# A hybrid decoder layer on one core: seven-product pairs in ten more column units, single wide splits, a denser state-space branch and branch results kept in DRAM

## The chip, the cores and the metric

The kernel runs on one core of a Trainium2 chip. Its engines are named as in the profile: PE (matrix multiply, with PEld for its weight loads), DVE (element-wise work on two inputs), ACT (element-wise work on one input, functions), POOL and SP; SP, ACT and POOL can issue DMAs, and each issues in the order of its own queue. The metric is the time of one execution in microseconds; the time of a kernel is the median of several.

## The reference

One decoder layer for 256 tokens of width 4096, in float32, and a final norm. What is computed, cut to its frame:

```python
def hybrid_layer(x, ln_g, w_in, ..., branch_g, w_out):
    h = rmsnorm(x, ln_g)
    proj = h @ w_in                                    # 4096 x 12288
    p_x, p_gate, q, k, v, a_gate, s_u, s_gate = split(proj)
    y_pool = pool_mixer(p_x, w_pool, pool_scale)       # causal pooling, 1024 wide
    y_attn = stick_breaking_attention(q, k, v)         # 16 heads, 2048 wide
    y_ssm = s5_mixer(s_u, ..., w_glu, b_glu)           # state space, 1024 wide, then GELU and h @ w_glu (1024 x 2048)
    y = concatenate([rmsnorm(y_pool, g_pool) * silu(p_gate),
                     rmsnorm(y_attn, g_attn) * silu(a_gate),
                     rmsnorm(y_ssm, g_ssm) * silu(s_gate)])
    return x + y @ w_out                               # 4096 x 4096
# and rmsnorm(., final_g) of the result
```

## The kernel before, in words

**Units and pairs.** The three weight matrices are cut into units of 512 columns: 24 of `w_in`, 4 of `w_glu`, 8 of `w_out`. `IN_ORDER` gives the order: two each of `su`, `px`, `pg`, `sg`; then `v`, `q`, `k` three times; the four `glu`; `v`, `q`, `k` once more; four `ag`; then eight `out`. A unit walks over its rows in pairs of 128-row blocks: 16 pairs in an `in` or `out` unit, 4 in a `glu` unit, 528 pairs in all (`N_SUB`). The weights of a pair, 512 KB, come by one DMA from SP into one of four buffers `w` (`load`).

**Three products for float32.** A pair's weights are split into a rounded part `hi` (ACT, a copy to fp32r) and a remainder `lo` (DVE, a subtraction), here one 128-row block (128x512) at a time, with five buffers each (`split`). The stationary operand, `xhl`, is split in the same way. `mm_tok` multiplies hi by hi, hi by lo and lo by hi for both halves of the tokens: 12 matmuls of 512 columns a pair.

**Seven products for four.** In the pairs 2, 5, 7, 9 and 11 of each `out` unit (`SEVEN`) the 2 x 2 block product over two token halves and two 256-column halves is formed from seven block products instead of eight. `sums_seven` makes four sums of weight blocks on DVE and splits them (`sums7`), one pair ahead of the pair's own split (`SUMS_AHEAD`); `split_seven` splits the raw blocks; `mm_seven` issues 7 x 3 matmuls of 256 columns; four of the seven go to PSUM tiles of their own, which `join_seven` adds up once a unit. Sums of the rows of `xhl` that they need are made by `sums_of_rows` during the last `ag` unit.

**Side work.** The state-space branch (`ssm`, on the DVE above all) and the other branches' work are generators. The main loop advances `side_q` by three steps a pair, and `ssm_q` by `SSM_RATE` = 1.5 steps a pair from pair 30 on; a scheduler that works offline turns the order in the program into a fixed order for each engine, and moves an instruction ahead of others where it expects it to be ready. SP is left out of that: its DMAs are issued in program order. Results of branches stay in SBUF: `ypT`, `ysT`, `yaT`, `ao`, `sgate`, `uT`.

**The hand-over to the output projection.** After the last `ag` unit, `finish` refills `xhl` with the branch results, one block at a time:

```python
if n == 3:
    for i in range(28):
        hi_lo(xhl[:, i, 0, :], xhl[:, i, 1, :], y_src(i))
```

A block can be refilled as soon as the last `ag` unit has used it. The four blocks left come straight from `att_gate`'s last call (`direct`).

**The end.** The last four pairs (`HELD`) are multiplied for the first token half at once and for the second half later, so that the first half's final norm lies beside matmuls.

Of the kernel before, what the change touches and what calls it, by code (L numbers as in the profile page):

```python
# [19 lines left out]
P = 128  # L20
L = 256
# [10 lines left out]
HELD = 4  # L32
WARM = 8
SUMS_AHEAD = 1
SEVEN = (2, 5, 7, 9, 11)
SQUARE_AT = (0, 1, 3, 4, 6, 7, 9, 10)
SSM_FROM = 30
SSM_RATE = 1.5
# [18 lines left out]
def body(tc, a, out, ctx):  # L57
    nc = tc.nc
    V, S, T = nc.vector, nc.scalar, nc.tensor
# [17 lines left out]
    bp = pool("base")  # L77
    pm = pool("pmain", space=PSUM)
# [14 lines left out]
    def act(o, x, f, **kw):  # L93
        S.activation(o, x, f, **kw)  # L94
# [8 lines left out]
    xt0 = bp.tile([P, 2, L], F32, tag="k4", bufs=6, name="xt")  # L103
# [25 lines left out]
    wtiles, htiles = {}, {}  # L129
    held = []  # L130
# [13 lines left out]
    def hi_lo(dst_hi, dst_lo, src):  # L144
        act(dst_hi, src, AF.Copy)
        tt(dst_lo, src, dst_hi.bitcast(F32), ALU.subtract)

    def seven(i):
        return i < N_SUB and subs[i][1] in SEVEN and units[subs[i][0]][0] == "out"

    def sums_seven(i):
        w = wtiles[i]
        left, right = w[:, :, 0:L], w[:, :, L:2 * L]
        t = bp.tile([P, 4, L], F32, tag="k4", bufs=6, name="t7")
        tt(t[:, 0:2, :], right, w[:, 0, :].rearrange("p (c m) -> p c m", c=2), ALU.subtract)
        tt(t[:, 2, :], right[:, 1, :], t[:, 0, :], ALU.subtract)
        tt(t[:, 3, :], left[:, 1, :], t[:, 2, :], ALU.subtract)
        sums = bp.tile([P, 2, 4, L], F32R, tag="k8", bufs=3, name="sums7")
        hi_lo(sums[:, 0], sums[:, 1], t)
        htiles[i] = sums  # L160

    def split_seven(i):
        w = wtiles.pop(i)
        raw = []
        for kk in range(2):
            n = L if kk == 0 else NU
            hi = wp.tile([P, NU], F32R, tag="hi", bufs=5, name="hi")
            lo = wp.tile([P, NU], F32R, tag="lo", bufs=5, name="lo")
            hi_lo(hi[:, 0:n], lo[:, 0:n], w[:, kk, 0:n])
            raw.append((hi, lo))  # L170
        htiles[i] = (raw, htiles[i])

    def mm_seven(i, s, ps, pp):
        (b11, b2), sums = htiles.pop(i)
        xa, xb, y = xhl[:, 2 * s], xhl[:, 2 * s + 1], state["s7"][s]
        lo_half, hi_half = slice(0, P), slice(P, L)
        first = s == SEVEN[0]
        last = s == SEVEN[-1]
        for o, stat, mov, begin, end in (
            (pp[0], xa[:, :, lo_half], [v[:, 0:L] for v in b11], first, last),  # L180
            (ps[:, 0, 0:L], xb[:, :, lo_half], [v[:, 0:L] for v in b2], False, False),
            (ps[:, 0, L:2 * L], y[:, 2], [v[:, L:2 * L] for v in b2], False, False),
            (pp[1], y[:, 0], [sums[:, h, 0] for h in range(2)], False, last),
            (pp[3], xa[:, :, hi_half], [sums[:, h, 1] for h in range(2)], first, last),
            (pp[2], y[:, 1], [sums[:, h, 2] for h in range(2)], False, last),
            (ps[:, 1, 0:L], xb[:, :, hi_half], [sums[:, h, 3] for h in range(2)], False, False),
        ):
            for k, (p, q) in enumerate(((0, 0), (0, 1), (1, 0))):
                T.matmul(o, stat[:, p, :], mov[q], start=begin and k == 0, stop=end and k == 2, skip_group_check=True)  # L189

    def join_seven(pp, xr):
# [839 lines left out]
```

## Time and profile before

| | |
|---|---|
| median of 3 runs | 1538.15 us (1537.11 to 1541.42) |
| the profiled execution | 1538.15 us, its span 1536.4 us |
| granted TensorE clock | 0.998 |
| PE busy | 1521.1 us |
| DVE busy | 1186.9 us |
| ACT busy | 931.6 us |
| moved by DMA | 308.22 MB, 201 GB/s on average |

Busy time is the union of an engine's instructions. A matmul's row shows the start and a modelled end; successive matmuls overlap, so what one costs is read from the distance of two starts. In a row of the list of waits stand the engine, line and tile that waited, what released it, and then the sum, the number and the longest of the waits in microseconds.

### The profile page before, as it was taken

To read this page: it belongs to the slowest core of one execution; us is meant where nothing else is said; L and a number is where in the kernel's file an instruction comes from. 1 tells how busy PE (TensorE), PEld (TensorE's weight loads), DVE (VectorE), ACT (ScalarE), POOL (GpSimd) and SP (SyncE) were. 2 spreads that over 40 slices of the span, in tenths; PEclk is the share of its full clock that TensorE was granted. 3 is DMA by queue.
4 is the path that set the end of the run, shared out by engine and by line. 5 is a ranking of instruction groups with operands and counts; after the bars stand their busy time and mean duration, and the time that the engine had idled before them with its cause. 6 is when DMAs were issued, how large, how long until landed. Compare 5 with 4: busy or idle time off the path is not lost.

```text
span 1536.4 us, 21621 instructions
## 1 busy us (share of the span) xinstructions
PE 1521.1 (99%) x7328; PEld 1266.3 (82%) x7328; DVE 1186.9 (77%) x2304; ACT 931.6 (61%) x1677; POOL 0.2 (0%) x4
## 2 busy tenths in 40 slices
PE   9999999999999999999999999999999999999996
PEld 7888788878788888788888888888888888888885
DVE  7579878999899879897645744555677988888886
ACT  7765556766566655575546755456677655555554
POOL 0000000000000000000000000000000000000000
PEclk9999999999999999999999999999999999999999
DMA  9866655665656556554655555555655666666665
GB/s 336 310 220 202 194 179 187 196 209 185 209 187 196 189 165 200 189 179 159 191 192 178 182 185 189 192 164 178 192 183 187 218 221 213 223 210 206 216 215 199
DMA packets 94351, 308.22 MB, mean 201 GB/s; under 512 B 11808, under 2 KB 17696, under 8 KB 94240
## 3 DMA queue, kind: packets, MB, share of 16 engines
q1 hardware_dynamic: 84096, 295.92, 58.5%
q10 hardware_dynamic: 10144, 10.92, 2.5%
q8 instruction: 57, 0.93, 0.3%
q14 instruction: 54, 0.44, 0.1%
HBM read 299.45 MB, written 4.19 MB: 198 GB/s over the span
## 4 chain that ended last, share of the span: by engine, by line
PE 96%; DVE 2%; DMA 1%; ACT 0%; issue 0%; SPq 0%; DVEq 0%; ACTq 0%
PE pm L242 29%; PE pm L241 28%; PE pm L243 28%; PE ps L189 3%; PE pm L189 2%; DMA w<-in_ws 1%; PE ps_y L562 1%; PE ps_c L658 1%; DVE lo L82 1%; PE ps_bu L535 1%; PE ps_z L588 0%; PE ps_p L346 0%; PE ps_t L286 0%; DVE t L82 0%; PE ps_z L606 0%; DVE sums L82 0%
## 5 line engine op out<-in xcount | busy, mean ns | idle before, releaser
L82 DVE TENSOR_TENSOR lo<-w,hi 128x512 fp32r<-128x512 f32 (+1 forms) x1048 | 697.5, 680 | 272.5 <-ACT hi L232 266.3
L232 ACT ACTIVATE hi<-w 128x512 fp32r<-128x512 f32 x968 | 602.3, 629 | 455.0 <-PE pm L243 270.0
L242 PE MATMUL pm<-lo,xhl 128*128 128x512 f32 x1872 | 732.7, 391 | 0.2 <-DVE lo L82 0.2
L241 PE MATMUL pm<-hi,xhl 128*128 128x512 f32 x1872 | 730.9, 391 | 1.1 <-ACT xhl L94 0.6
L243 PE MATMUL pm<-hi,xhl 128*128 128x512 f32 x1872 | 731.0, 391 | 0.0
L241 PEld LDWEIGHTS pm<-hi,xhl 128*128 128x128 f32 x1872 | 351.8, 188 | 75.1 <-ACT hi L232 1.7
L242 PEld LDWEIGHTS pm<-lo,xhl 128*128 128x128 f32 x1872 | 351.8, 188 | 74.4 <-issue 2.9
L243 PEld LDWEIGHTS pm<-hi,xhl 128*128 128x128 f32 x1872 | 351.8, 188 | 71.2 <-issue 0.8
L91 DVE SCALAR_TENSOR_TENSOR et<-et,pw,tr 128x16 f32<-128x16 f32 (+3 forms) x256 | 56.2, 277 | 1.5 <-ACT tr L94 1.3
L94 ACT ACTIVATE sums<-t 128x1024 fp32r<-128x1024 f32 x40 | 42.3, 1057 | 24.6 <-DVE t L82 24.6
L82 DVE TENSOR_TENSOR sums<-t,sums 128x1024 fp32r<-128x1024 f32 x40 | 48.9, 1223 | 9.2 <-ACT sums L94 9.2
L94 ACT ACTIVATE hi<-w 128x256 fp32r<-128x256 f32 x80 | 40.0, 518 | 23.4 <-PE pm L243 19.7
L94 ACT ACTIVATE tr<-et,pw 128x32 f32<-128x32 f32 (+3 forms) x128 | 45.4, 386 | 9.6 <-DVE et L91 5.5
L189 PE MATMUL ps<-sums,s 128*128 128x256 f32 x240 | 46.8, 285 | 0.9 <-DVE sums L82 0.9
L82 DVE TENSOR_TENSOR t<-w 128x512 f32<-128x512 f32 x40 | 27.6, 690 | 22.0 <-DMA w<-in_ws 21.9
L550 DVE TENSOR_TENSOR_SCAN tb<-rho,ta 128x256 f32<-128x256 f32 x64 | 40.7, 680 | 0.1
L189 PEld LDWEIGHTS ps<-sums,s 128*128 128x128 f32 x240 | 36.7, 192 | 1.7 <-DVE sums L82 1.5
L82 DVE TENSOR_TENSOR t<-w,t 128x256 f32<-128x256 f32 x80 | 33.7, 421 | 0.3
L94 ACT ACTIVATE sgm<-sgm 128x1024 f32<-128x1024 f32 x24 | 25.3, 1052 | 0.2
L243 PE MATMUL pm<-hi,hhl 128*128 128x512 f32 x64 | 25.3, 395 | 0.0
L242 PE MATMUL pm<-lo,hhl 128*128 128x512 f32 x64 | 25.2, 393 | 0.0
L241 PE MATMUL pm<-hi,hhl 128*128 128x512 f32 x64 | 25.1, 392 | 0.0
(259 smaller groups left out, 1123.7 us busy)
## 6 DMA issues: line engine op xcount, KB each, us to landing
w<-in_ws SPq DMA_DIRECT2D x527, 512.0 KB, 3.4
xsq<-in_xr SPq DMA_DIRECT2D x8, 512.0 KB, 6.5
xr<-in_xr SPq DMA_DIRECT2D x8, 512.0 KB, 4.5
xt<-in_xT SPq DMA_DIRECT2D x15, 256.0 KB, 6.0
b<-in_bst ACTq DMA_DIRECT2D x16, 192.0 KB, 3.8
u<-uT ACTq DMA_DIRECT2D x96, 32.0 KB, 2.6
out<-o SPq DMA_DIRECT2D x6, 512.0 KB, 4.1
fg<-in_fg SPq DMA_DIRECT2D x8, 256.0 KB, 5.5
```

The source lines that it names most:

```text
L82: V.tensor_tensor(o, x, y, op)
L91: V.scalar_tensor_tensor(o, x, s, y, op0, op1)
L94: S.activation(o, x, f, **kw)
L189: T.matmul(o, stat[:, p, :], mov[q], start=begin and k == 0, stop=end and k == 2, skip_group_check=True)
L232: made = S.activation(hi, w[:, kk, :], AF.Copy)
L241: T.matmul(ps[t], stat[:, slot, 0, sl], hi, start=first, stop=False)
L242: T.matmul(ps[t], stat[:, slot, 0, sl], lo, start=False, stop=False)
L243: T.matmul(ps[t], stat[:, slot, 1, sl], hi, start=False, stop=last)
L535: T.matmul(ps[:, c, :], b3r[:, j, c, :], u3r[:, j, :], start=c == 0, stop=True, skip_group_check=True)
L550: V.tensor_tensor_scan(tb[:, c, :], rho[:, pr:pr + 1].broadcast_to([P, L]), ta[:, c, :], 0.0, ALU.mult, ALU.add)
L562: T.matmul(ps[32 * j:32 * j + 32, 0:L], cf[:, j, c, :], ss[j][:, c, :], start=c == 0, stop=c == 1, skip_group_check=True)
L658: T.transpose(ps[:, (c * 2 + t) * P:(c * 2 + t + 1) * P], z[:, t, (h * 2 + c) * P:(h * 2 + c + 1) * P], ident)
```

## The change

1. Seven-product pairs: six of 16 pairs, in each `out` unit (`SEVEN_OUT`) and now also in the `in` units from the fifteenth on (`SEVEN_IN`, `SEVEN_FROM`): the last two groups of `v`, `q`, `k` and the four `ag`, ten units. For these the rows' sums come from `x`, loaded again (`load_again`, `sums_of_x`) during the unit before. The four separate PSUM tiles of an `in` unit take the second buffers of the main PSUM tiles.
2. The last `v`, `q`, `k` group moves ahead of `glu`. `SSM_RATE` becomes 1.75, and the state-space branch must be complete at the start of unit 13 (`start_late`; unit 16's end before).
3. A pair is split in one instruction of ACT and one of DVE (128x1024), in a ring of four buffers (`RING`); the sums of a seven-product pair take a second buffer of the ring and are split when the pair is, no longer one pair ahead. The sums themselves are made one pair ahead, as before.
4. Branch results go to DRAM from POOL's queue (`kept`, `aout`, `sgate`) and come back: seven groups by `take_back` from SP after the last `ag` unit, with the rows' sums made there; the others from POOL.
5. Main PSUM tiles are one per token half. The tail scales the output in four pieces instead of five; the held pairs stay in the ring.

```diff
+RING = 4
+K4 = 8
 SUMS_AHEAD = 1
-SEVEN = (2, 5, 7, 9, 11)
+SEVEN_FROM = 14
+SEVEN_IN = (0, 3, 5, 8, 10, 12)
+SEVEN_OUT = (1, 3, 6, 8, 10, 12)
-SSM_RATE = 1.5
+SSM_RATE = 1.75
+    + [("v", V0 + 1536), ("q", Q0 + 1536), ("k", K0 + 1536)]
     + [("glu", n) for n in (1024, 0, 1536, 512)]
-    + [("v", V0 + 1536), ("q", Q0 + 1536), ("k", K0 + 1536)]
...
+    def ring():
+        return [wp.tile([P, 4 * L], F32R, tag=k, bufs=RING, name=k) for k in ("hi", "lo")]
...
     def sums_seven(i):
+        w = wtiles[i].rearrange("p k n -> p (k n)")
+        b12, b11, b22, b21 = (w[:, q * L:q * L + L] for q in range(4))
+        t = bp.tile([P, 4, L], F32, tag="k4", bufs=K4, name="t7")
+        tt(t[:, 0, :], b12, b11, ALU.subtract)
+        tt(t[:, 1, :], b22, b12, ALU.subtract)
+        tt(t[:, 2, :], b22, t[:, 0, :], ALU.subtract)
+        tt(t[:, 3, :], b21, t[:, 2, :], ALU.subtract)
+        stiles[i] = t
+    def split(i):
...
+        w = wtiles.pop(i).rearrange("p k n -> p (k n)")
+        raw = ring()
+        at = L if seven(i) else 0
+        for n in (slice(0, NU), slice(NU, 2 * NU)) if i == 0 else (slice(at, 2 * NU),):
+            made = hi_lo(raw[0][:, n], raw[1][:, n], w[:, n])
+        if seven(i):
+            sums = ring()
+            hi_lo(sums[0], sums[1], stiles.pop(i).rearrange("p q m -> p (q m)"))
...
+        for o, stat, mov, start, stop in (          # mm_seven
+            (pp[0], xa[:, :, lo_half], b11, begin, False),
+            (pp[1], y[:, 0], t0, False, end),
+            (pp[3], xa[:, :, hi_half], t1, begin, False),
+            (pp[2], y[:, 1], t2, False, end),
+            (ps[0][:, L:2 * L], xb[:, :, lo_half], b21, first, False),
+            (ps[0][:, 0:L], y[:, 2], b22, False, False),
+            (ps[1][:, L:2 * L], xb[:, :, hi_half], t3, first, False),
...
+    def row_sums(s, xa, xb):
+        t = state["rows"].tile([P, 3, P], F32, tag="t", bufs=1, name="ts")
+        tt(t[:, 0, :], xa[:, P:L], xb[:, P:L], ALU.add)
+        tt(t[:, 1, :], t[:, 0, :], xa[:, 0:P], ALU.subtract)
+        tt(t[:, 2, :], xb[:, 0:P], t[:, 1, :], ALU.subtract)
+        y = state["rows"].tile([P, 3, 2, P], F32R, name="y7_%d" % s)
+        hi_lo(y[:, :, 0, :], y[:, :, 1, :], t)
+    def row_difference(xa):
+        tt(xa[:, P:L], xa[:, 0:P], xa[:, P:L], ALU.subtract)
+    def sums_of_x(s):
+        xs = xtiles.pop(s)
+        for j in range(2):
+            act(xs[:, j, :], xs[:, j, :], AF.Copy, scale=ln_g[:, 2 * s + j:2 * s + j + 1])
+        row_sums(s, xs[:, 0, :], xs[:, 1, :])
+        row_difference(xs[:, 0, :])
+        hi_lo(xhl[:, 2 * s, 0, P:L], xhl[:, 2 * s, 1, P:L], xs[:, 0, P:L])
+    def take_back(g):
+        t = bp.tile([P, 4, L], F32, tag="k4", bufs=K4, name="yk")
+        nc.sync.dma_start(t, kept[g])
+        for h in range(2):
+            s = 2 * g + h
+            if s in SEVEN_OUT:
+                row_sums(s, t[:, 2 * h, :], t[:, 2 * h + 1, :])
+                row_difference(t[:, 2 * h, :])
+        hi_lo(xhl[:, 4 * g:4 * g + 4, 0, :], xhl[:, 4 * g:4 * g + 4, 1, :], t)
...
     def scaled(ps, name):
+        e = state.pop("joined", None)
+        if e is not None:
+            times_r(e, [e[:, t, :] for t in range(2)])
+            tt(z, z, e, ALU.add)
...
             if n == 3:                               # finish, "ag"
-                for i in range(28):
-                    hi_lo(xhl[:, i, 0, :], xhl[:, i, 1, :], y_src(i))
+                for g in range(7):
+                    take_back(g)
...
+            if ui == SEVEN_FROM - 1:                 # main loop, s == 0
+                start_late()
+                state["rows"] = lp
+        if these and s == these[0]:
+            if kind != "out":
+                pz = [pm.tile([P, 2, L], F32, tag="c%d" % t, bufs=2, name="p7") for t in range(2)]
```

More of the change, by code (lines that the diff above doesn't have):

```diff
@@ L162, in split_seven @@
[L162 to L174, printed above, removed]
+        if i >= N_SUB:
+            return False
@@ L247, in body @@
+    state = {"s7": {}}
     xtiles = {}
@@ L363, in pool_gate, with uT @@
         y = ypool.pop(u)
[L364 to L368 removed]
+        yield from transposed(y, keep(u))
+    u_parts = [bp.tile([P, 4, L], F32, tag="k4", bufs=K4, name="uT") for _ in range(2)]
+    def uT(ct):
+        return u_parts[ct // 4][:, ct % 4, :]
+    glu, sgate = {}, {}
     def ssm_params(sp, k):
@@ L738, in start_end @@
         state["o"] = ep.tile([P, 2, D], F32, name="o")
-    def y_src(i):
-        return ypT[:, i, :] if i < 8 else state["ysT"][:, i - 8, :] if i < 16 else state["yaT"][:, i - 16, :]
     def start_out(n):
```

321 lines of the change are left out of this document (146 added, 175 removed).

## The prediction

> **What bounds the kernel now.** First the page's busy times, then the list of waits of PE alone, whole.
>
> ```profile
> span 1536.4 us, 21621 instructions
> PE 1521.1 (99%) x7328; PEld 1266.3 (82%) x7328; DVE 1186.9 (77%) x2304; ACT 931.6 (61%) x1677; POOL 0.2 (0%) x4
> ```
>
> ```profile
> PE ps_i L111 <- DVE zeros L108: 1.2, 1, 1.2
> PE ps L189 <- DVE sums L82: 0.9, 2, 0.5
> PE pm L241 <- DVE o L82: 0.8, 1, 0.8
> PE pm L241 <- ACT xhl L94: 0.6, 1, 0.6
> ...
> PE pm L242 <- DVE lo L82: 0.2, 1, 0.2
> ```
>
> PE is fed from end to end: it waits some 4 us in 1536. So a cut in PE's work counts in full as long as DVE, ACT and the weight DMAs keep delivering, and what they cannot deliver comes back as a wait of PE. How much room they have is read stage by stage (busy time of PE, PEld, DVE, ACT, POOL in each stretch, then clock and DMA):
>
> ```profile
> 100.00:735.00 635.00, 635.00 (x2963) 518.28 (x2963) 559.03 (x1251) 387.68 (x720) 0.00 (x0) 1.00 0.59 189
> 735.00:1137.00 402.00, 402.00 (x1849) 334.91 (x1848) 230.87 (x357) 233.15 (x391) 0.00 (x0) 1.00 0.58 185
> 1180.00:1222.50 42.50, 41.98 (x239) 36.77 (x238) 37.59 (x64) 28.13 (x47) 0.00 (x0) 1.00 0.63 209
> 1307.50:1350.00 42.50, 42.50 (x238) 37.20 (x237) 36.13 (x59) 24.67 (x42) 0.00 (x0) 1.00 0.66 216
> ```
>
> The rows are the stage with the state-space branch, the input units behind it, the first output unit and a later one. DVE is at 88%, 57%, 88% and 85%; ACT has room everywhere. DVE is the engine that can become the bound.
>
> **1. The added seven-product pairs.** What a matmul costs is the distance of starts:
>
> ```profile
> 1420.08 0.28 PE L189 MATMUL ps<-sums,xhl 128*128 128x256 f32 x1
> ...
> 1421.76 0.52 PE L189 MATMUL pm<-sums,xhl 128*128 128x256 f32 x3
> ...
> 1430.60 0.39 PE L243 MATMUL pm<-hi,xhl 128*128 128x512 f32 x1
> ...
> 1439.67 0.39 PE L241 MATMUL pm<-hi,xhl 128*128 128x512 f32 x1
> ```
>
> Between the first two rows lie 14 starts, 1.68/14 = 0.120 us for 256 columns; between the last two 40 starts, 9.07/40 = 0.2268 us for 512. A plain pair is 12 x 0.2268 = 2.722 us, a seven-product pair 21 x 0.120 = 2.520: 0.202 us saved, 7%, not an eighth, because 256 columns cost more than half of 512. Before there are 8 x 5 = 40 such pairs, after it 8 x 6 + 10 x 6 = 108. 68 x 0.202 = 13.7 us. That is the whole gain; the other edits make room for it. (Between 13 and 14.5, if the distances move by 1%.)
>
> The Trainium skill, "TensorE: Matmul & The Clock Gate", section "Back-to-back issue gap", gives N/2.4 + 2.5 ns for isolated warm matmuls. By it the distances would be 109 and 216 ns, a pair would save 0.29 us and the 68 pairs 20 us. The trace disagrees: 0.120 and 0.2268 are both about 11 ns over that formula, which 21 matmuls pay more often than 12, so the measurement decides.
>
> **2. DVE's bill for them.** DVE instructions too are priced by the distance of starts:
>
> ```profile
> 1405.46 1.23 DVE L82 TENSOR_TENSOR sums<-t,sums 128x1024 fp32r<-128x1024 f32 x1 [0.19 <-ACT sums L94]
> 1406.60 0.69 DVE L82 TENSOR_TENSOR t<-w 128x512 f32<-128x512 f32 x1
> 1407.20 0.69 DVE L82 TENSOR_TENSOR lo<-w,hi 128x512 fp32r<-128x512 f32 x1
> 1407.80 0.42 DVE L82 TENSOR_TENSOR t<-w,t 128x256 f32<-128x256 f32 x1
> 1408.14 0.69 DVE L82 TENSOR_TENSOR lo<-w,hi 128x512 fp32r<-128x512 f32 x1
> ```
>
> 1024 columns cost 1.14 us, 512 cost 0.60, 256 cost 0.34; so some 0.07 each and 0.267 for 256 columns, and by estimate from these 0.87 for 768, 0.47 for 384, 0.20 for 128. A plain pair's remainder falls from 1.20 to 1.14. A seven-product pair costs 4 x 0.34 + 0.87 + 1.14 = 3.37 (before: 0.60 + 2 x 0.34 + 1.14 + 0.60 + 0.34 = 3.36). An output unit is then 10 x 1.14 + 6 x 3.37 = 31.6 against 11 x 1.20 + 5 x 3.36 = 30.0 before: +1.6 on 36.13, so 37.7 in a unit that PE does in 42.3, 89%. An input unit with six pairs has 31.6 and the joining, 4 x 0.34 + 1.14 = 2.5, and its side work: 57% becomes some 85%. On average DVE holds, and this step costs nothing by itself.
>
> **3. The shorter warning for sums.** Their split moves behind the pair's own and shares a ring of four. Where two such pairs stand two apart (3, 8, 10, 12 of an output unit; 5, 10, 12 of an input unit: 8 x 4 + 10 x 3 = 62 cases) the sums' buffer is the one that the raw blocks of the former pair free three matmuls before that pair ends, and the sums are wanted after three matmuls of the next one: 0.36 + 2.72 + 0.36 = 3.44 us for ACT's split and DVE's.
>
> ```profile
> L94 ACT ACTIVATE sums<-t 128x1024 fp32r<-128x1024 f32 x40 | 42.3, 1057 | 24.6 <-DVE t L82 24.6
> L94 ACT ACTIVATE kz<-pm,rtok 128x512 f32<-128x512 f32 x8 | 5.1, 686 | 2.2 <-PE pm L243 2.2
> ```
>
> 1.06 + 1.23 leave 1.15 us; a single ACT instruction of 1.06 us ahead uses that up. Nothing to 0.4 us a case, 0 to 25 us. I take 1 us in all, near the lower end: before, the same sums made PE wait twice in 40 pairs (0.9 us).
>
> **4. PSUM of the input units.** The separate tiles take the second buffers, so at ten unit starts pair 0 or its like waits until ACT has emptied the unit before: the second token half is emptied after the unit's last matmul, 0.69 us (row of `kz`). Six matmuls of the first token half's tiles (0.72 us) and, in an order that the scheduler may choose, nine on the main tiles can run ahead of it. 0 to 10 x 0.69 = 7 us; I take 1, since the matmuls ahead cover the evacuation unless ACT is late.
>
> **5. The hand-over to the output units.** Here the change moves work onto the path. Before, the refill of `xhl` runs inside the last input unit, block by block behind PE:
>
> ```profile
> 1138.15 0.42 DVE L82 TENSOR_TENSOR xhl<-ypT,xhl 128x256 fp32r<-128x256 f32 x1
> ...
> 1175.85 0.42 DVE L82 TENSOR_TENSOR xhl<-yaT,xhl 128x256 fp32r<-128x256 f32 x1
> ```
>
> ```profile
> 1179.91 1.27 ACT L94 ACTIVATE agz<-pm,rtok 128x512 f32<-128x512 f32 x2 [0.15 <-PE pm L243]
> ```
>
> All 28 blocks are nearly done when that unit ends (`agz`, 1179.9). After the change the data must come back first, and `take_back`'s seven DMAs stand on SP behind the weights of the fourth output pair, whose buffer comes free only when the last input pair is split.
>
> ```profile
> w<-in_ws SPq DMA_DIRECT2D x527, 512.0 KB, 3.4
> SPq L141 <- DVE lo L82: 1037.3, 423, 6.6
> ```
>
> SP waits there in nearly every pair. That split waits for the ring buffer which pair 12 frees, three plain pairs or 8.2 us before the end; the first group is issued some 5.8 us before it and lands, with 3.4 us, 2 to 3 us before it. So nearly all the work falls into the first output unit: 7 x 1.14 + 6 x (3 x 0.20 + 0.47 + 0.20) = 15.6 us of DVE. With the 37.59 us that DVE does in this unit now and 1.6 more, it is 54.8 us against 42.3: 12.5 too many. Against it stand the lead of the ring (two to three pairs, some 4 us of DVE work that may be eaten up) and one group done early (2.4): 6 us are left for PE to wait. From 0 (all refills find gaps) to 13 (no lead, and the seven loads, which hold the next weights back on SP, land late). I take 6, the sum.
>
> **6. The state-space branch.** It must end before pair 224, when unit 14's first pair needs its space. Before:
>
> ```profile
> 665.98 1.27 ACT L94 ACTIVATE kz<-pm,rtok 128x512 f32<-128x512 f32 x2 [0.73 <-PE pm L243]
> ```
>
> ```profile
> L82 DVE TENSOR_TENSOR uT<-y,l x8: 418/420/422, 192.8 to 738.3; 128x256 f32<-128x256 f32 x8
> ```
>
> Unit 13 ends at 666, the branch at 738: 72 us too late. The same stretch, `lo` alone:
>
> ```profile
> 100.00:735.00 635.00, 331.67 (x847) 158.96 (x846) 286.58 (x423) 1.00 0.59 189
> ```
>
> 423 half pairs in 635 us are 3.0 us a pair, so 24 pairs too late. Its 10 + 8 x 37 = 306 steps take 204 pairs of the order at 1.5 and 175 at 1.75: 29 pairs earlier, 5 to spare (15 us), from which come the first rows' sums (under 2 us). DVE in that stage: 286.58 of `lo` in 211.5 pairs is 1.36 a pair and becomes 1.30; the rest, 272.45, is 1.29 a pair and becomes x 1.167 = 1.50; 2.80 of 3.0 us, 93% for 88%. 0 to 15 us, as the branch keeps its place or falls 10 pairs further behind; I take 1.
>
> **7. The ends.** At the start a pair can only begin when all its 1024 columns are split:
>
> ```profile
> 8.30 1.15 ACT L232 ACTIVATE hi<-w 128x512 fp32r<-128x512 f32 x2 [0.59 <-DMA w<-in_ws]
> ```
>
> ACT's second 512 columns cost 0.52 there, DVE's 0.54 more: 0 to 1.1 us, I take 0.7. At the end PE now waits for the reading of the other token half's tile:
>
> ```profile
> 1518.37 0.39 PE L243 MATMUL pm<-held,xhl 128*128 128x512 f32 x1
> ...
> 1519.54 0.50 PE L241 MATMUL pm<-held,xhl 128*128 128x512 f32 x1 [0.78 <-DVE o L82]
> ```
>
> 1.17 less 0.23: 0.9 us, gone with a tile per half. Three held pairs instead of four leave less cover (1.36 us) for the first half's norm: -0.9 to +0.5; I take -0.9. The stores and loads through DRAM (some 15 MB on 308) and POOL's queue have no reader that is near, apart from `take_back`.
>
> **Sum.** The profiled execution, 1538.15 us with 1.75 us outside its span, is the median itself. 1538.15 - 13.7 + 1 + 1 + 6 + 1 + 0.7 - 0.9 = 1533.25.
>
> **The rivals.** *The hand-over costs nearly all it can* (step 5 at its upper end, 10 to 13, and PE running without lead in the next unit): 1537 to 1541, within what a measurement can tell, which is 0.3% or 4.6 us. For it: 12.5 us of overload, and the present unit has PE waits already. Against it: the scheduler knows of the overload and can spread it. *Slower: the state-space branch is late.* Its place is the first pair of unit 14, whose rows' sums lie in the branch's space; each pair of further lag past the 5 to spare holds PE 3 us. With the other losses as taken it decides from 3 to 4 late pairs on (10 us): 1543 and over. For it: the branch already ran 13 to 14 pairs behind its place, on a DVE at 88%. Against: once PE is held, DVE is free for the branch. *The hand-over is hidden after all* and little else is lost: 1538.15 - 13.7 + 2 = 1526 to 1529; for it speaks that ACT and PE show no wait at the present one. *A full eighth is saved*, if 256 columns cost half of 512 once such pairs stand closer: 0.113 instead of 0.120 us, 0.34 a pair, 23 us, 1524 with the losses as taken; the 14 starts quoted above are already back to back, which speaks against it. The page of the Trainium skill named in step 1 lies between, with 20 us.
>
> **How the numbers follow.** The forecast's case, some 3 to 8 us gained, 0.37, with its own range of 1530 to 1535; hidden hand-over 0.25; dear hand-over 0.20; late branch or the short warnings of step 3 at over 0.2 us a case 0.17; the full eighth 0.01. From 1525 to 1542 holds 8 in 10. Below 1533.5 lie the hidden case and two thirds of the forecast's: 0.5; between 1533.5 and 1542.8: 0.32; above: 0.18.
>
> **What would show it.** Starts 0.120 us apart in 108 pairs; PE's waits in the first output unit, on `xhl` and on `lo`, some 6 us, with DVE dense from its start; the last `agz` at 1168 (60 x 0.202 earlier) plus whatever was lost before; no PE wait at the start of unit 14, the last `uT` before it; PE's wait on `o` at the end gone. Wrong it would be if PE waits a few tenths at most seven-product pairs, or if the branch's last write comes after unit 13's end.

## The result and the profile after

The changed kernel takes 1629.21 us (median of four runs, 1628.55 to 1632.80) against 1537.82 us before (four runs, 1537.11 to 1541.42): ratio 1.0594, 95% interval 1.0571 to 1.0617. It is 91.4 us slower; 1525 to 1542 was forecast. The profiled execution took 1629.87 us, its span 1628.1.

The head of the page, with the busy shares of PE and DVE, the granted clock and the transfer rate over 40 slices of 40.7 us each:

```profile
span 1628.1 us, 22047 instructions
...
PE 1540.8 (95%) x7940; PEld 1298.0 (80%) x7940; DVE 1324.2 (81%) x2230; ACT 926.0 (57%) x1246; POOL 10.5 (1%) x23
...
PE   9999999999999997299999999999998899999996
PEclk9999999999999998599999999999999999999998
GB/s 345 304 206 205 189 190 199 191 227 207 194 196 197 186 190 106 20 224 144 196 201 139 201 198 207 162 235 193 198 175 251 194 201 225 210 218 211 221 208 182
```

One hole stands out: in the seventeenth slice PE is at 2 and the DMAs move 20 GB/s. The list of PE's waits, where before some 4 us stood in all:

```profile
PE ps_bu L567 <- DVE tb L88: 16.4, 2, 11.5
PE p L211 <- ACT hi L100: 13.5, 6, 2.8
PE ps_y L594 <- DVE tb L88: 9.4, 1, 9.4
PE ps_y L594 <- DVE s L88: 7.3, 3, 3.4
PE pm L241 <- ACT xhl L100: 6.2, 2, 5.6
PE pm L242 <- DVE lo L88: 5.6, 7, 1.0
```

First, third and fourth row are the state-space branch (`ps_bu`, `ps_y`): PE waits at the branch's own matmuls, because nothing else is ready. The second row is the sums of seven-product pairs in input units (`p`), the fifth the hand-over (`xhl`).

To place the loss I add up, stretch by stretch, how far the starts of successive matmuls stand apart beyond their steady distances (0.2268 us for 512 columns, 0.120 for 256): 16.6 us before, 115.6 after. Of the latter, 48.1 lie between 625 and 700 us, 33.5 between 725 and 1250 (the input units with seven-product pairs), 18.4 between 1250 and 1325 (the first output unit and the start of the second), 6.4 in the first 25 us (before: 3.9), and nothing worth naming in the output units that follow. The sums depend on what counts as steady: with the median distance of every shape as the steady one they are 33.2 before and 134.3 after, 51.1, 36.7, 18.4 and 4.7 in the four stretches. Less what the kernel before loses in the same stretches (3.2, 4.9, 0.9 and 2.3), the losses agree with those above within 2 us.

Windows of 50 us round the hole (PE, PEld, DVE, ACT and POOL busy, then clock, DMA share, GB/s), and a stretch of output units:

```profile
600.00:650.00 50.00, 42.09 (x210) 33.77 (x208) 33.91 (x66) 22.83 (x37) 0.53 (x1) 0.93 0.34 110
650.00:700.00 50.00, 19.58 (x67) 12.57 (x68) 41.31 (x93) 21.36 (x44) 0.00 (x0) 0.56 0.22 78
...
1350.00:1600.00 250.00, 250.00 (x1445) 220.99 (x1444) 219.37 (x322) 137.34 (x159) 0.00 (x0) 1.00 0.67 219
```

The granted clock follows the stall and is not its cause: in the trace's record it drops to 0.5 at 642.9 us, 5 us after PE ran dry, and comes back at 694.1, some 6 us after the main matmuls start again. The same happens behind shorter waits. One wait of the second row in the list (2.8 us) ends at 752.5; the stretch behind it:

```profile
752.50:759.00 6.50, 6.46 (x21) 5.62 (x22) 6.48 (x9) 5.25 (x6) 0.00 (x0) 0.50 0.63 187
```

PE has work all the time, but matmuls of 512 columns start 0.427 us apart instead of 0.2268. Of the eight waits over 1.4 us outside the hole, seven are followed by 3.4 or 6.8 us at a granted clock of 0.5 (half clock); in the kernel before, the record is at 0.5 only behind the last matmul. By the count with median distances, some 24 of the 134 us are slow starts of this kind with no wait beside them: 7.9 in the stretch of the hole, 9.6 in the input units, 4.8 at the hand-over, 1.4 at the start. So a wait of PE costs more than itself, and none of the prediction's steps has a term for it.

What DVE does in the hole, and what SP has issued by then (timeline):

```profile
626.87 1.22 DVE L88 TENSOR_TENSOR lo<-w,hi 128x1024 fp32r<-128x1024 f32 x1
638.08 0.69 DVE L652 COPY ao<-ps_av 128x512 f32<-128x512 f32 x1 [9.99 <-PE ps_av L650]
...
687.68 0.48 DVE L97 SCALAR_TENSOR_TENSOR y<-uT,prm,ps_y 128x256 f32<-128x256 f32 x1 [1.67 <-PE ps_y L594]
688.08 1.22 DVE L88 TENSOR_TENSOR lo<-w,hi 128x1024 fp32r<-128x1024 f32 x1
```

```profile
596.64 17.15 SPq L146 DMA_DIRECT2D w<-in_ws  x6
618.52 0.33 SPq L262 DMA_DIRECT2D xs<-in_xT  x1
642.58 3.02 SPq L146 DMA_DIRECT2D w<-in_ws  x3
```

Between two splits of weights, at 626.87 and 688.08, DVE does nothing but the state-space branch and one copy for the attention. On SP the first reload of `x` (`xs`, `load_again`) goes out at 618.52, and the weights behind it only at 642.58. What SP waited for (600 to 720 us, two rows of its list):

```profile
SPq L146 <- DMA u<-uT: 26.2, 3, 23.7
SPq L262 <- PE ps_z L623: 1.8, 1, 1.8
```

The reload itself (`L262`) waited 1.8 us, for matmuls of the attention. The weights behind it (`L146`) waited 23.7 us for `u<-uT`, a DMA of the state-space branch that ACT issues at 640.71 and that counts on the same semaphore in the trace. These weights land at 647.2, and even then their split is not next in the order of ACT:

```profile
686.02 1.04 ACT L100 ACTIVATE hi<-w 128x1024 fp32r<-128x1024 f32 x1
```

So weights are missing for the first 9 us of the hole; for the 39 us behind, they lie there, and what holds PE is the fixed order of ACT and DVE, in which the split stands behind the branch. Of DVE, 99 other instructions stand between the 214th and the 215th split, in the built program and in the trace alike; the longest such run in the kernel before has 13.

### The profile page after: what moved, and what is told of

Read it like the earlier page. It is cut to its first block, busy times and chain, and to the rows that moved or that the text cites. A ratio compares the mean times of both kernels' runs of the same rounds, so it can differ in the third digit from the quotient of the medians.

```text
span 1628.1 us, 22047 instructions
## 1 busy us (share of the span) xinstructions
PE 1540.8 (95%) x7940; PEld 1298.0 (80%) x7940; DVE 1324.2 (81%) x2230; ACT 926.0 (57%) x1246; POOL 10.5 (1%) x23
## 4 chain that ended last, share of the span: by engine, by line
PE 88%; DVE 6%; DMA 3%; ACT 2%; issue 1%; SPq 0%; DVEq 0%; ACTq 0%
PE pm L242 23%; PE pm L241 23%; PE pm L243 23%; PE pm L211 6%; PE p L211 5%; PE ps L211 4%; DMA w<-in_ws 2%; DVE lo L88 2%; PE ps_y L594 1%; ACT hi L100 1%; DVE ta L88 1%; DVE t L88 1%; PE ps_c L692 0%; PE ps_p L376 0%; DVE xhl L88 0%
## 5 line engine op out<-in xcount | busy, mean ns | idle before, releaser
L100 ACT ACTIVATE hi<-w 128x1024 fp32r<-128x1024 f32 (+2 forms) x529 | 532.4, 1012 | 378.4 <-PE pm L243 308.4
L88 DVE TENSOR_TENSOR lo<-w,hi 128x1024 fp32r<-128x1024 f32 (+2 forms) x529 | 612.0, 1165 | 130.2 <-ACT hi L100 128.0
L242 PE MATMUL pm<-lo,xhl 128*128 128x512 f32 x1616 | 638.3, 395 | 5.7 <-DVE lo L88 5.6
L243 PE MATMUL pm<-hi,xhl 128*128 128x512 f32 x1616 | 635.3, 393 | 0.0
L241 PE MATMUL pm<-hi,xhl 128*128 128x512 f32 x1616 | 622.8, 395 | 9.0 <-ACT xhl L100 6.2
L100 ACT ACTIVATE hi<-t 128x1024 fp32r<-128x1024 f32 x108 | 114.3, 1059 | 100.0 <-DVE t L88 59.5
L88 DVE TENSOR_TENSOR lo<-t,hi 128x1024 fp32r<-128x1024 f32 x108 | 131.9, 1222 | 26.9 <-ACT hi L100 26.8
L88 DVE TENSOR_TENSOR t<-w 128x256 f32<-128x256 f32 x216 | 82.0, 422 | 65.8 <-DMA w<-in_ws 65.6
L211 PE MATMUL pm<-hi,xhl 128*128 128x256 f32 x432 | 119.3, 285 | 0.0
L211 PE MATMUL p<-hi,y 128*128 128x256 f32 x240 | 66.2, 288 | 13.5 <-ACT hi L100 13.5
L211 PE MATMUL p<-hi,xhl 128*128 128x256 f32 x240 | 66.1, 285 | 0.0
```

Source lines behind the costliest of these rows:

```text
L88: V.tensor_tensor(o, x, y, op)
L100: return S.activation(o, x, f, **kw)
L211: T.matmul(o, stat[:, p, :], mov[q], start=start and k == 0, stop=stop and k == 2, skip_group_check=True)
L241: T.matmul(ps[t], stat[:, slot, 0, sl], hi[:, n], start=begin, stop=False, skip_group_check=True)
L242: T.matmul(ps[t], stat[:, slot, 0, sl], lo[:, n], start=False, stop=False, skip_group_check=True)
L243: T.matmul(ps[t], stat[:, slot, 1, sl], hi[:, n], start=False, stop=end, skip_group_check=True)
```

## The experiments

In the expectations TensorE is PE, VectorE DVE, ScalarE ACT, SyncE SP and GpSimd POOL. The kernel before, run beside each, took 1537.6 to 1538.4 us; all ratios are to it. "Run" of other instructions means the longest one between two splits on DVE in the built program.

**The reload from another queue.**

```diff
-        nc.sync.dma_start(xs, a["xT"][s])
+        G.dma_start(xs, a["xT"][s])
```

> The six reloads of x for the rows' sums (load_again) are issued from GpSimd instead of SyncE; all else as in the changed kernel. In the built program the longest run of other VectorE instructions between two splits of weights moves from behind split 214 (99 instructions) to behind split 226 (90). Theory A (the branch must end before the first seven-product pair, 224, and is late there whoever loads x): TensorE's dry stretch of some 50 us moves from pair 213 to pair 224 and gets shorter by what the branch can do beside the ten pairs gained; 15 to 45 us of it remain, total 1595 to 1626. Theory B (the reload holds SyncE's queue, and with it the weights): the dry stretch is gone, 1629 - 48 = 1581.

1620.55 us, ratio 1.0541 (1.0525 to 1.0557): 8.7 us less than the changed kernel. The hole moves from 638 to 670 us and 38 us of it are left. Where PE runs dry depends on SP's queue; that it runs dry does not.

**Fewer input units.**

```diff
-SEVEN_FROM = 14
+SEVEN_FROM = 17
```

> Seven-product pairs begin at input unit 17 instead of 14 (seven units with six each instead of ten). The state-space branch then has until pair 272 instead of 224. Theory A (deadline of the branch): the dry stretch at 638 to 688 us is gone (-48), 18 pairs less save 3.6 us less, and the two stalls at the start of units 15 and 18 are one fewer (-3): 1578 to 1584. Theory C (the seven-product pairs of the input units themselves overload the feeding engines, and the dry stretch is a part of that): only the three units' share is saved, 1610 or more.

1579.15 us, ratio 1.0265 (1.0249 to 1.0280): 50 us less, as theory A says. The hole is gone. At this point "the branch is late for pair 224" seemed settled, but this run moves two things at once: the deadline, and the place where `load_again` and the sums first ask for buffers.

**The old rate with the new deadline.**

```diff
-SSM_RATE = 1.75
+SSM_RATE = 1.5
```

> The branch is emitted at 1.5 steps a pair as in the kernel before, the seven-product pairs still from unit 14. In the built program two runs of VectorE instructions stand between splits, 33 behind split 214 and 89 behind split 224, 122 against 99. Theory A, with the denser emission doing what it is meant to: the stall grows by the 29 pairs' delay, some 20 to 85 us, 1650 or more. Theory D (the denser emission does not make the branch faster, since its pace is set by the chain of its own operations): the same within 10 us, 1620 to 1640.

1623.09 us, ratio 1.0556 (1.0540 to 1.0572). Theory D's number; the denser emission earns nothing here. The rest of the branch is now put into the program in one go at pair 208, which brings a hole by another way.

**No seven-product pairs in input units.**

```diff
-SEVEN_FROM = 14
-SEVEN_IN = (0, 3, 5, 8, 10, 12)
+SEVEN_FROM = 20
+SEVEN_IN = ()
```

> No seven-product pairs in input units at all; the output units keep six of sixteen, the results still go through DRAM and come back at the hand-over. If my reading of the trace after adds up: 1538 - 8 x 0.202 (1.6) - 0.9 (end) + 2.5 (start) + 18 (first two output units) = 1556. If the losses at the hand-over come from the seven-product pairs of the last input unit (no free VectorE time ahead of it), it falls to 1538 to 1545.

1560.39 us, ratio 1.0152 (1.0135 to 1.0169). This is 4 us over the expected 1556, and far from the rival's 1538 to 1545: the hand-over is dear even with plain input units ahead of it. And the pairs of the seven input units in the run from unit 17 do not save 42 x 0.202 = 8.5 us, they cost 1579.2 - 1560.4 = 19.

**The hand-over spread out** (on top of `SEVEN_FROM = 17`).

```diff
-                for g in range(7):
-                    take_back(g)
...
+        if ui == 27 and s % 2 and s < 14:
+            take_back(s // 2)
```

> As the run that begins at unit 17 (1579.15), but the seven groups come back one by one inside the last input unit, each behind the pair that reads its rows of xhl last, instead of all at that unit's end. Theory H (the hand-over is dear because its VectorE work, some 15.6 us, and the loads fall into the first output unit): TensorE's waits at the first two output units, some 14 us in that run's trace, fall to under 5; total 1566 to 1570. Rival (VectorE is as full in the last input unit as in the first output unit, so the work only moves): within 4 us of 1579.

1567.05 us, ratio 1.0184 (1.0167 to 1.0201): 12.1 us gained, theory H. In the traces PE's waits in the first two output units fall from 11.6 to 4.1 us, while those in the last input unit rise from 2.5 to 4.3. The same window, first without, then with the change:

```profile
1200.00:1250.00 50.00, 40.80 (x207) 34.52 (x208) 44.35 (x79) 30.24 (x38) 0.54 (x1) 0.86 0.54 195
```

```profile
1200.00:1250.00 50.00, 45.84 (x250) 38.87 (x249) 46.22 (x74) 34.60 (x42) 0.00 (x0) 0.97 0.58 209
```

**The first pair of input units** (on top of `SEVEN_FROM = 17`).

```diff
-SEVEN_IN = (0, 3, 5, 8, 10, 12)
+SEVEN_IN = (1, 3, 6, 8, 10, 12)
```

> As the run that begins at unit 17, but the seven-product pairs of an input unit are 1, 3, 6, 8, 10, 12 instead of 0, 3, 5, 8, 10, 12. Theory U (the stalls of 2.3 to 3 us at the first pair of input units, where ScalarE splits the sums behind the unit's side work, come from a seven-product pair standing at the unit's very start): six such stalls go, 10 to 14 us, total 1565 to 1569. Rival (whatever the first pair is, it waits there): within 4 us of 1579.

1579.71 us, ratio 1.0269 (1.0254 to 1.0284): no change, theory U falls. Four of the five stalls moved with the third seven-product pair of the unit (5, here 6), not with the first; the fifth, in unit 17, moved from pair 8 to pair 6. I had misread their place: in the trace after, ACT stands 3.73 us at the evacuation of the transposes of the unit before, with the split of the sums (`hi<-t`) behind it in its order:

```profile
1122.96 1.57 ACT L100 ACTIVATE yT<-ps_t,prm 128x256 f32<-128x256 f32 x4 [3.73 <-PE ps_t L299]
1124.40 1.07 ACT L100 ACTIVATE hi<-t 128x1024 fp32r<-128x1024 f32 x1
```

**The end** (on top of `SEVEN_FROM = 17`).

```diff
+            if kind == "out" and c == 7:
+                both = pk.tile([P, 2, NU], F32, tag="pz", bufs=1, name="pm_both")
+                ps = [both[:, t, :] for t in range(2)]
```

> As the run that begins at unit 17, but the last output unit's two token halves stand in one PSUM tile, as in the kernel before, so that the held matmuls of the second half come behind the reading of the first. Theory T (with a tile for each half the scheduler mixes the held matmuls in, both halves end together, and all stores stand behind the last matmul): from the last matmul to the end 16.4 us becomes about 11.5, total 1574. Rival (the stores' size, 1024 columns instead of 512 first, makes the longer end): 16 us stay, 1579.

1573.98 us, ratio 1.0236 (1.0221 to 1.0251): 5.2 us, theory T. The reading of the two halves in the changed kernel, then here:

```profile
1610.74 0.69 DVE L88 TENSOR_TENSOR o<-pm,xr 128x512 f32<-128x512 f32 x1 [2.88 <-PE pm L243]
1612.10 0.69 DVE L88 TENSOR_TENSOR o<-pm,xr 128x512 f32<-128x512 f32 x1 [0.67 <-PE pm L243]
```

```profile
1559.66 0.69 DVE L88 TENSOR_TENSOR o<-pm_both,xr 128x512 f32<-128x512 f32 x1 [0.15 <-PE pm_both L243]
...
1564.86 0.69 DVE L88 TENSOR_TENSOR o<-pm_both,xr 128x512 f32<-128x512 f32 x1 [0.20 <-PE pm_both L243]
```

1.4 us apart in the one, 5.2 in the other: with a tile for each half nothing keeps the held matmuls behind the first half's reading, and the scheduler mixes them in.

**The sums' lead** (on top of `SEVEN_FROM = 17`).

```diff
-SUMS_AHEAD = 1
+SUMS_AHEAD = 0
```

> As the run that begins at unit 17, but the sums of a seven-product pair are formed right before that pair's split, not one pair ahead. Theory W (VectorE's queue is held where the sums wait for weights that have just been asked for, 2 to 3 us at a time): those waits go and the input units from 17 on gain, 1570 or less. Rival (the sums' lead is needed: ScalarE's split of the sums then comes later and TensorE waits more): 1585 or more.

1584.93 us, ratio 1.0301 (1.0285 to 1.0318): 5.8 us more; the lead is needed.

**A space of their own for the rows' sums, at both rates.** `SEVEN_IN = (0, 5, 10)` makes room for a pool beside the branch's; `start_late` moves to unit 19, so that the branch has no deadline before it. The second kernel has `SSM_RATE = 1.4` besides.

```diff
-            if ui == SEVEN_FROM - 1:
-                start_late()
-                state["rows"] = lp
+            if ui == 19:
+                start_late()
+            if ui == SEVEN_FROM - 1:
+                state["rows"] = rows_in
```

> As the changed kernel, seven-product pairs from input unit 14, but with three of them a unit (0, 5, 10), which leaves room for the rows' sums in a space of their own; the branch's space is wanted only at unit 19, so the branch has no deadline at pair 224 any more. Rate 1.75 as in the change. Theory A1 (space: the rows' sums must wait for the branch's space): no dry stretch, 1629 - 48 + 6 (30 seven-product pairs fewer), and up to 15 less for lighter input units: 1572 to 1587. Theory A2 (order: at 1.75 steps a pair the branch is written into the program far ahead of where the engines are; the side work written behind it waits for the two small PSUM buffers that it holds, and the first load that wants a buffer of that side work, the reload of x, then stands on SyncE ahead of the weights): the dry stretch at pair 213 stays as it is, some 50 us, 1615 to 1635. The built program has 103 other VectorE instructions in one run between splits 214 and 215 (the changed kernel: 99).

> As the run with a space of their own for the rows' sums, but with the branch emitted at 1.4 steps a pair instead of 1.75 (the engines carried out some 1.46 in the changed kernel). Theory A2 (order): the dry stretch is gone, 1572 to 1587; the longest run of other VectorE instructions between two splits falls from 103 to 16. If the lateness of the branch itself were the cause, wherever it is wanted, the stretch would be as long or longer, 1615 or more.

1620.34 us, ratio 1.0534 (1.0518 to 1.0550), and 1574.53 us, ratio 1.0237 (1.0222 to 1.0252). This overturns my theory: without the deadline the hole stays, and with a slower emission it goes. Rate alone is worth 46 us. The window of the hole, at 1.75 and at 1.4:

```profile
650.00:700.00 50.00, 21.52 (x76) 14.13 (x77) 45.06 (x102) 22.23 (x45) 0.00 (x0) 0.58 0.21 74
```

```profile
650.00:700.00 50.00, 50.00 (x261) 40.51 (x261) 46.05 (x91) 32.69 (x51) 0.00 (x0) 1.00 0.53 178
```

DVE is as busy in both (45 and 46 us). What differs is the order: between two splits stand up to 103 other instructions in the first trace and up to 22 in the second.

**Without pair 5** (on the spread hand-over).

```diff
-SEVEN_IN = (0, 3, 5, 8, 10, 12)
+SEVEN_IN = (0, 3, 8, 10, 12)
```

> As the run from unit 17 with the groups coming back one by one (1567.05), but without the seven-product pair 5 of each input unit, at which TensorE waits 2.3 to 3 us in six of seven units: there ScalarE stands at the evacuation of the transposes of the unit before, and behind it the split of the sums. Theory V (it is this meeting of the two at pair 5): 7 x 0.202 = 1.4 less saved, 11 us of waits gone: 1556 to 1560. Rival (the wait moves to the next seven-product pair, 8): 1565 to 1570.

1563.39 us, ratio 1.0163 (1.0148 to 1.0178): 3.7 us, between the theories. The expectation counts six stalls at pair 5; the trace of the run without this edit shows four there and one at pair 8 (1.5 to 2.8 us). Of these five, three are left, one of them grown to 3.5 us. Which order of side work and sums would be free of them stays open.

**Plain input units with both mends.** The edits of three runs above together: `SEVEN_IN = ()`, the groups back one by one, one PSUM tile at the end.

> The run without seven-product pairs in input units (1560.39), with the groups coming back one by one and with the one PSUM tile at the end. If the terms add up: 1560.4 - 12 - 5.2 = 1543, still some 5 above the kernel before. If the two mends overlap, up to 1550; if VectorE, idle in the last input unit here, hides all of the hand-over, 1538 or less.

1546.11 us, ratio 1.0051 (1.0035 to 1.0068). The terms add up to within 3 us, and 8 us remain against the kernel before, of which 4.5 at the hand-over.

**A buffer of its own for the reload** (on the run with a space of its own, rate 1.75).

```diff
-        xs = bp.tile([P, 2, L], F32, tag="k4", bufs=K4, name="xs")
+        xs = bp.tile([P, 2, L], F32, tag="xs", bufs=1, name="xs")
```

> As the run with a space of their own for the rows' sums (rate 1.75, 1620.3), but the reloaded x has a buffer of its own instead of one of the ring of eight that the side work shares. Theory A3 (the ring is the link: the reload waits there for side work that is written behind the branch): the weights pass, the dry stretch starts some ten pairs later, where the sums of the first seven-product pair want a buffer of the same ring, and is shorter; 1595 to 1612. In the built program the longest run is 75 instructions behind split 226 instead of 103 behind split 214. Rival (the reload is held by SyncE or by its transfer, not by the ring): as before, 1615 to 1625.

1596.28 us, ratio 1.0382 (1.0366 to 1.0398): 24 us less, and the hole begins at 670 us. With a buffer of its own for the reload, the weights behind it no longer stand on SP:

```profile
612.37 0.43 SPq L262 DMA_DIRECT2D xs<-in_xT  x1
614.47 14.86 SPq L146 DMA_DIRECT2D w<-in_ws  x5
```

So the ring `k4` is a link, and it is worth about half of the 46 us. The longest run of other instructions is now 77 in the trace, from 662.14 to 696.71 us. That the second user of the ring on the main path, the sums `t7`, makes this rest (22 us over the run at 1.4) fits its place, but no run gives these sums a buffer of their own. Why the ring moves the splits is inferred too: the scheduler seems to expect a longer wait for the ring's buffer than the 1.8 us of the trace, and to write the splits of the weights behind it accordingly late. The traces show only the order that it made.

**The denser rate alone**, in the kernel before.

```diff
-SSM_RATE = 1.5
+SSM_RATE = 1.75
```

> The kernel before with 1.75 steps a pair instead of 1.5 and nothing else. Theory A2/A3 (the denser emission is harmful only where the main path wants a buffer of the ring, which no main-path instruction of the kernel before does in that stretch): 1536 to 1541, no dry stretch, and the branch's last result moves from 738 us by less than 25 us, since its pace is that of its own chain, and not by the 87 us that 29 pairs would be. If the rate set the pace: last result near 650 us.

1543.19 us, ratio 1.0036 (1.0022 to 1.0049). No hole, as expected, but 5.4 us lost, with no wait of PE to show for it, and a branch that ends 55 us earlier, not under 25: the time and the shift both missed.

**Six input units, everything mended**: the kernel at 1.4 with a space of its own, the spread hand-over and the mended end, and

```diff
-... SEVEN_IN if kind != "glu" and ui >= SEVEN_FROM else ()
+... SEVEN_IN if kind not in ("glu", "ag") and ui >= SEVEN_FROM else ()
```

It leaves out restoring the rows of `xhl`: its `ag` units multiply by the differences that the seven-product pairs left there, which is not what the reference computes, and the time of restoring them is missing from its own.

> Branch at 1.4 with the rows' sums in their own space, three seven-product pairs (0, 5, 10) in the six input units 14 to 19, none in the four gate units, groups back one by one, one PSUM tile at the end. From the run without seven-product pairs in input units and both mends (1546.1): 18 x 0.202 = 3.6 saved, 1542.5 if they cost nothing. If each unit start still costs 1 to 3 us: 1546 to 1556. Below 1538 only if the lower rate gives something too.

1542.18 us, ratio 1.0032 (1.0019 to 1.0044). 18 pairs would save 3.6 us against 1546.1, and 3.9 came; but the rate differs too, so this is no clean proof that these pairs pay.

**One visit for a channel tile.** The 5.4 us of the rate alone came without a wait, so I looked at what PE does in the rows of the branch's output matmuls (`ps_y`, groups by line, with all shapes apart): busy time, mean ns of one, for the kernel before and for the rate alone.

```profile
L562 PE MATMUL ps_y<-s,cf 128*32 128x256 f32 x128 | 14.7, 389 | 0.0
```

```profile
L562 PE MATMUL ps_y<-s,cf 128*32 128x256 f32 x128 | 18.4, 390 | 0.0
```

The same 128 matmuls, but in more groups between the main ones: 18 and 24, in the built programs and in the traces. In the kernel before a group of four and one of ten look so:

```profile
176.06 0.63 PE L562 MATMUL ps_y<-s,cf 128*32 128x256 f32 x4
176.61 0.50 PE L242 MATMUL pm<-lo,xhl 128*128 128x512 f32 x1
...
185.82 0.39 PE L243 MATMUL pm<-hi,xhl 128*128 128x512 f32 x1
186.13 1.05 PE L562 MATMUL ps_y<-s,cf 128*32 128x256 f32 x10
187.12 0.50 PE L241 MATMUL pm<-hi,xhl 128*128 128x512 f32 x1
187.45 0.39 PE L242 MATMUL pm<-lo,xhl 128*128 128x512 f32 x1
```

Going in costs 0.31 us and coming out 0.33 where 0.2268 is the rule: some 0.2 us in all. The rest is the group itself. From its first start to the next main matmul a group of two, four or six takes some 0.55 us, one of ten 0.98 and one of sixteen 1.00, so many small groups cost more than a few large ones. The edit, in the kernel before and in the mended one without seven-product input pairs, moves the forming of `cf` behind the four states, so that all sixteen matmuls of a channel tile become ready together:

```diff
-            cf = sp.tile(...)                # ahead of the four states
-            tt(c1, cr, ...); tt(c2, cr, ...); tt(cf[...], ...); stt(cf[...], ...)
...
+            cf = sp.tile(...)                # behind them, same four instructions
+            tt(c1, cr, ...); tt(c2, cr, ...); tt(cf[...], ...); stt(cf[...], ...)
             ps = pk.tile([P, 512], F32, tag="ps", bufs=2, name="ps_y")
```

> The kernel before, with the state-space branch's output coefficients (cf) formed after its four states instead of ahead of them, so that the sixteen output matmuls (ps_y, 32 columns of the array each) of a channel tile start together: the built program has 8 groups of them between the main matmuls instead of 18. Theory S (each change between the main matmuls and these and back costs some 0.8 us: 5.1 us for 6 to 7 visits more in the run with the rate alone): 10 fewer save 8 us, 1530. Rival (the 5 us of that run are contention elsewhere, spread over the stretch): 1536 to 1540.

1530.33 us, ratio 0.9951 (0.9937 to 0.9964): 8.05 us faster than the kernel before, theory S, and the fastest of all runs. In the traces the groups themselves take 13.4 us before and 8.0 here; with 0.2 us at the borders of each of the ten groups that are gone this makes 7.4 of the 8.05. For the six more groups of the rate alone it makes 4.5 of the 5.4. Its row:

```profile
L562 PE MATMUL ps_y<-s,cf 128*32 128x256 f32 x128 | 8.6, 385 | 0.0
```

> The run without seven-product pairs in input units, with the groups coming back one by one and one PSUM tile at the end (1546.1), and the branch's output coefficients formed late as well: 9 groups of output matmuls instead of 23 in the built program. Theory S: 14 fewer at 0.8 save 11 us, 1535. Rival: 1544 to 1548.

1543.94 us, ratio 1.0040 (1.0027 to 1.0052): only 2.2 us, and the single times overlap (1542.7 to 1546.0 here, 1544.8 to 1547.0 without the edit). The excess between 100 and 600 us falls by 8 to 9 us, but PE now waits 7.5 us at the last channel tile (its matmuls start at 711.6 us), where the coefficients come late, and the excess between 600 and 760 us grows by about as much.

## Why the prediction was wrong

The step that failed is **step 6**, the state-space branch, in its size and in its mechanism. It took 1 us and bounded the cost at 15; 48 us stand there. Three things in it were wrong.

The first is the pace. "Its steps take 175 pairs at 1.75: 29 pairs earlier" takes the rate of emission for the rate of execution. The first and the last `y` of the branch (view of the tile's instructions: first and last start) in the kernel before, the rate alone, the run from unit 17, and the run at 1.4:

```profile
L91 DVE SCALAR_TENSOR_TENSOR y<-uT,prm,ps_y x8: 475/480/481, 187.2 to 732.2; 128x256 f32<-128x256 f32 x8
```

```profile
L91 DVE SCALAR_TENSOR_TENSOR y<-uT,prm,ps_y x8: 472/479/481, 188.2 to 677.4; 128x256 f32<-128x256 f32 x8
```

```profile
L97 DVE SCALAR_TENSOR_TENSOR y<-uT,prm,ps_y x8: 472/481/481, 189.6 to 717.2; 128x256 f32<-128x256 f32 x8
```

```profile
L97 DVE SCALAR_TENSOR_TENSOR y<-uT,prm,ps_y x8: 474/481/481, 205.1 to 778.3; 128x256 f32<-128x256 f32 x8
```

A seventh of each span is 77.9, 69.9, 75.4 and 81.9 us a channel tile. At 3.0 us a pair 37 steps would be 74 us at 1.5, 63 at 1.75 and 79 at 1.4. At 1.4 and 1.5 the branch keeps up within 4 us a tile; at 1.75 it does not. The run from unit 17, asked for 63, does 75; the kernel before, with its narrower splits, does 70 at the same rate. The narrow splits are the likely difference, but that was not tried by itself. DVE's 93%, estimated in the same step, was no room for a chain of operations in which each needs the result of the one ahead.

The second is the place. The prediction had the first pair of unit 14 wait for the branch's space. The hole is at pair 213, eleven pairs earlier, and it stays without that space (run with a space of its own). What stands there is the split of the weights, behind the branch in the fixed order of DVE and ACT. For about half of the hole the cause is shown: the reload of `x` takes its buffer from a ring shared with side work that is written behind the branch (run with a buffer of its own). The other half is laid to the sums `t7` in the same ring, which was not tried by itself. The whole hole goes when the branch is emitted at 1.4. Step 5 did ask what the seven loads of `take_back` hold back on SP; the same question for the six of `load_again` was never put, though step 6 was the place for it.

The third is the size. "Each pair of further lag holds PE 3 us", and "once PE is held, DVE is free for the branch". The branch alone, on a free DVE, still needs 40 us for a channel tile (`y` at 647.4 and 687.7). The rival *slower: the branch is late* named the right branch and gave 1543 and over, at a chance of 0.17 that it shared with step 3's short warnings, but with the wrong place; and step 6 capped its price at 15. Of the 48 us, 7.9 are matmuls at half clock, for which the step has no term.

**Step 1** held. In the trace after, steady starts of the seven-product pairs lie 0.12 us apart:

```profile
1444.70 0.28 PE L211 MATMUL ps<-hi,xhl 128*128 128x256 f32 x1
...
1445.65 0.28 PE L211 MATMUL pm<-lo,y 128*128 128x256 f32 x1
```

0.95 us for 8 starts, and the six steady output units take (1570.47 - 1317.06)/6 = 42.24 us each, forecast 42.3. The step's bracket of 13 to 14.5 us was too narrow for its condition, since 1% of the 256-column distance alone moves the gain by 1.7. The formula of the Trainium skill named there (109 ns) is again not met. **Step 2** held: DVE is at 81% on average and at 88% in the output units (forecast 89%), where its load alone makes no loss. **Steps 3 and 4** were too small: 2 us taken, 33.5 in the input units, a little over their upper ends together (25 and 7). Six stalls of 1.5 to 2.8 us make 13.5 of it; there ACT's order has the side work's evacuation (of transposes in four, of attention scores in two) ahead of the sums' split. The row that I bounded by (one ACT instruction of 1.06 us ahead) did not allow for an ACT that itself waits for PE first. Some 9.6 us more are matmuls at half clock behind these stalls; the rest are small distances that I did not take apart. **Step 5** had the right mechanism: DVE's work at the hand-over, 12.5 too many for the unit, less leads; it took 6, the excess there is 18.4 (bound 13; 10.6 in the list of waits, 4.8 at half clock), and spreading the same work over the unit before gives 12 of it back. **Step 7**: the head cost 2.5 instead of 0.7 in this execution (over the sixteen traces with this start the first 25 us lose 2.7 to 5.1 us, over the three with the old one 2.3 to 2.7), the end 4.9 instead of -0.9 (16.4 us from the last main matmul to the end of the span, 11.5 before); the wait on `o` that it did away with was what kept the held matmuls back.

Terms: -13.7 + 48.1 + 33.5 + (18.4 - 1.7, the excess already there before) + 2.5 + 4.9 = 92.0; measured 91.4. Not in this sum, and partly hidden in the hole, are the extra visits of `ps_y` (22 groups against 18).

## What to carry to other kernels

Where a scheduler fixes each engine's order, the rate at which side work is written into the program is no request for speed. Here it was written faster than its chain could run; one load on the main path that asked a shared ring for a buffer was then enough for an order with 99 side instructions between two splits, which the engines kept even when the weights had landed. So for each load or tile that a change adds to the main path, ask whose buffers it takes and what is written ahead of it. Price a wait of PE with the half clock that may follow it. And where PE is busy to the end, count how often it goes back and forth between shapes of matmul: that loss shows in no wait.

## What the runs showed of the hardware

Each further group of 32-column matmuls set between full ones cost 0.8 to 0.9 us at the same number of matmuls and with no wait recorded: 10 groups fewer saved 8.05 us, 6 more cost 5.4. Of this some 0.55 us is the group itself, for two to six matmuls alike, and 0.2 us lies at its borders (0.31 and 0.33 us against 0.2268). The Trainium skill, "TensorEngine Tiling (Array Packing)", section "Key Properties", says that changing the tiling mode drains TensorE. The rows above fit it: the full matmul behind the group of ten starts 0.06 us ahead of the group's modelled end, while full ones, 0.39 us long and 0.2268 apart, overlap by 0.16.

In the changed kernel seven of the eight waits of PE over 1.4 us outside the hole were followed by 3.4 or 6.8 us at a granted clock of 0.5, in which 512 columns took 0.427 us instead of 0.2268.
